# Late division in six 2-D attention heads, and the last two gate tiles as an eighth pair of block products

## The chip, the cores and the metric

The kernel runs on one core of one Trainium2 chip. The metric is the time of one execution on the device in microseconds (us); lower is better. The core has five engines that work through their own instruction lists in order: TensorE (PE, matrix products and transposes), VectorE (DVE), ScalarE (ACT), GpSimd (POOL) and SyncE (SP), which here only issues transfers (DMA). ACT issues some transfers too.

## The reference

One layer of an encoder on a sequence of 1024 positions of width 1024, all in float32. Two attentions with 8 heads of width 64 each run side by side on one projection of the same input, and their outputs are gated and summed:

```
h = rmsnorm(x) * (1 + scale1) + shift1
qa, ka, va, qb, kb, vb, ga, gb = split(h @ w_in)        # 6 x 512, then 2 x 1024 columns
oa = mixture_of_dilations(qa, ka, va)                   # 8 heads, 1-D windows
ob = neighbourhood_attention_2d(qb, kb, vb)             # 8 heads, 8 x 16 windows on a 16 x 64 grid
merged = sigmoid(ga) * (oa @ w_branch_dil) + sigmoid(gb) * (ob @ w_branch_na)
x = x + gate1 * (merged @ w_out)
...                                                     # then an up projection, a convolution, a down projection
```

In the 2-D attention each query row has its scores, a bias and a softmax over its window: `p = exp(s - max) / sum`, and `o = p @ v`. The division by the sum can stand before the product with v or behind it.

## The kernel before

Every product in full precision is made of three matmuls on halves of its operands: each float32 matrix is split into a high part (an ACT copy to a shorter format) and a low part (a subtraction on DVE or POOL), and high x high, high x low and low x high are summed in PSUM. The output of the projection is made transposed, in tiles of 128 columns of `w_in` by two halves of 512 positions. `w_in` has 40 such tiles; 24 to 39 are the gates.

The profiled execution falls into these stages (times from the trace):

- 0 to 143 us: the conditioning vector, the norm, and the products for the values.
- 143 to 276 us: the **block products**. Tiles of `w_in` are taken two at a time, as a pair, and the pair's product with `h` is made by a scheme with seven instead of eight block products (`STEPS`, `a_operands`, `products`). Seven pairs (`order = (4, 5, 6, 7, 1, 2, 3)`, the q and k tiles of both attentions) have 7 x 4 x 3 = 84 matmuls each. Their operands are sums and differences of blocks of the raw tiles, made by POOL and DVE and split by ACT and POOL while the pair before multiplies. Results leave PSUM through ACT and DVE (`na_evict`, `qk_evict`) into a tile `qs`, and from there go to `q_scr` in DRAM (the transfers `qks<-qs`).
- 276 to 282 us: nine units of the gates, as cover for the start of the attention.
- 282 to 610 us: the **attention**, a loop over slots numbered 0 to 101. Each slot has at most one block of scores `S` (PE), the transposes `T` of earlier softmax results (PE), and the products `O` with the values (PE). Slots 0 to 63 start the scores of the first attention, slots 64 to 95 those of the 2-D heads, four slots for each head (`NaHead(head, 64 + 4 * head)`). Between these PE does the gates as filling (`fill_steps`): 16 tiles of 2 halves of 8 units, where a **unit** is the three matmuls of lines L84, L85 and L86. The loop's number `n` says how many units a slot gets: 2 up to slot 63, 3 from 64 to 95, 1 behind. One unit stands ahead of S, the rest behind it. What is left comes behind the last slot.
- 610 to 710 us: the two branch products and the gating; then the output projection and the feed-forward part, which the change doesn't touch.

**One 2-D head.** The queries come in four blocks `cb`, in the order 0, 3, 1, 2, one a slot; I call these slots j = 0 to 3. Line L1260 makes two score matrices (R = 0, 1) of 128 queries by 288 keys (blocks 0 and 3) or 384 keys (1 and 2). Two slots of PSUM hold them. At the start of the next slot, `settle` runs the softmax: DVE adds the bias and takes the maximum (L1270), ACT takes the exponential and the row sums into `st[:, 1]` (L1272). Two slots behind the scores, `normalise` divides: DVE takes the reciprocal of two columns of sums (L1277), then POOL multiplies the R = 0 half of `P` and DVE the R = 1 half (L1280). Then PE transposes `P` in groups of four 128-column pieces (`turn`, L1289): per head six groups, in slots with two groups, one group, two groups, one group. The tile `T` has two PSUM banks. Each group leaves its bank through `split_t`: ACT copies the high part `th` (L878), DVE subtracts the low part `tl` (L882), and only then is the bank free.

The order inside `settle` is this: first all `th` copies of the turned groups (ACT), then the softmax of the scores just made (DVE, ACT), then the `tl` subtractions (DVE). So `tl` stands behind the softmax on DVE. `out` (L930) multiplies `th` and `tl` with the values, and an ACT copy (L1309) and a DVE addition (L1313) bring the result into `oTs[pair]`, a tile 128 x 1024 for two heads, which goes to `o_scr` in DRAM.

Other work of DVE, ACT and POOL in this stretch is queued with `aside(ns, one, two)` and handed out by `catch_up(550)` behind each unit: the splits of the gate weights (`whi` L961, `wlo` L962), of the values (`vv` L783, L784), the copies of finished gates (`gs`), the additions into `u`. SP's issues are written in the same slots: `bias`, `qs`, `ks`, `kl`, `vv` of a head come one head ahead; SP also carries the spreading of the merge weights of the first attention (`sts`, `fs`, `fcs`, `fb`), which ends in the first half of the 2-D heads.

Of the kernel before, what the change touches and what calls it, by code (L numbers as in the profile page):

```python
# [29 lines left out]
def hybrid_encoder(tc, xT, c, w_ada, small, w_in, p1_bias, p23_bias, na_bias, ln2_mult, ident, w_br, w_out,  # L30
# [8 lines left out]
    def f(ap):  # L39
        return ap.bitcast(FT)  # L40
# [240 lines left out]
    g_scr = dram.tile([16, 128, S], FT, name="gs")  # L281
    st_scr = dram.tile([4, 64, 128], FT, name="sts")
    f_scr = dram.tile([4, 2, 2, 8, S], FT, name="fcs")
    o_scr = [dram.tile([4, 128, S], FT, name=n) for n in ("oa", "ob")]
    v_scr = dram.tile([S + 9 * 128, 512], FT, name="v")
    va_s, va_b = v_scr[:S], v_scr[S:].rearrange("(j p) n -> j p n", j=9)
# [92 lines left out]
    def na_evict(pr, y, hf, p):  # L379
        first = (pr, y) not in na_st  # L380
        if first:
            na_st[pr, y] = [qkpool.tile([128, S], FR, name="qs") for _ in range(2)]
        st = na_st[pr, y]
        if y:
            split_qk(y, [t.rearrange("p (w t r) -> p r w t", w=16, t=16)[:, 2 * hf:2 * hf + 2] for t in st],
                     p.rearrange("p (r w t) -> p r w t", r=2, w=16))
        else:
            for r in range(2):
                split_qk(y, [t.rearrange("p (c w r t) -> p r c w t", c=4, w=16, r=4)[:, 2 * hf + r] for t in st],
                         p.rearrange("p (r w c t) -> p r c w t", r=2, w=16, c=4)[:, r])  # L390
        if not first:
            for x_, t in enumerate(na_st.pop((pr, y))):
                act.dma_start(q_scr[pr, 2 * y + x_], f(t))

    def qk_load(head):
        pr, i = divmod(head, 2)
# [129 lines left out]
    with tc.manual_schedule(engines={e.engine for e in (sp, act, dve, pool, pe)}):  # L526
# [176 lines left out]
            for c, d in ((c0, d0), (c1, d1)):  # L703
                pool.tensor_tensor(c, c, d, OP.subtract)

        order = (4, 5, 6, 7, 1, 2, 3)

        def p_load(n):
            pr, r = order[n], []
            for t in (pr, 4 + pr) if pr < 4 else (8 + pr, 12 + pr):  # L710
                r.append(wpool.tile([128, KT, 128], FT, name="wraw") if n % 2 == 0 and n < 6 else
                         lpool.tile([128, KT, 128], FT, name="xr", bufs=2))
                sp.dma_start(r[-1], w_in[t])
            return [t.rearrange("p (a b) m -> p a b m", a=2) for t in r]
# [95 lines left out]

    def p_products(n, seq=range(7)):
        pr = order[n]
        return products(p_sts[n], 4, p_moving, lambda i, hf, src: na_evict(pr, i, hf, src) if pr > 3 else
                        qk_evict(pr, i, hf, src, "qs"), seq, in_psum=True, other=lambda: p_spot([128, 2, 512])[:, 0])

    def advance(g):
        for j in g:
# [389 lines left out]
    class NaHead:  # L1207
        def __init__(self, head, s0):
            self.head, self.i = head, head % 2
            self.a = slice(64 * self.i, 64 * self.i + 64)  # L1210
            self.P, self.t3, self.bt = {}, {}, {}
            at(57 if head == 0 else s0 - 4, "first", lambda: qks.update({8 + head: qk_load(8 + head)}))
            at(s0, "first", self.begin)
            at(s0 + 2, "first", self.load)
            at(s0 + 6, "first", self.output)
            at(s0 + 5, "first", self.prepare)
            for n, cb in enumerate((0, 3, 1, 2)):
                at(s0 + n - 2, "first", self.bias, cb)
                at(s0 + n, "S", self.scores, cb)
                at(s0 + n + 2, "first", self.normalise, cb)  # L1220
            for n, pair in enumerate(((0, 3), (1, 2))):
                s = s0 + 4 + 2 * n
                for y in range(3):
                    at(s + (y == 2), "T", self.turn, pair, y)
                at(s + 3, "O", self.out, pair)
# [49 lines left out]
        def normalise(self, cb):  # L1275
            st, P, kn = self.st, self.P[cb], 48 * NA_NC[cb]
            dve.reciprocal(st[:, 1, 2 * cb:2 * cb + 2], st[:, 1, 2 * cb:2 * cb + 2])  # L1277
            for R in range(2):
                pp = P[:, R, :kn]
                (pool, dve)[R].tensor_scalar(pp, pp, st[:, 1, 2 * cb + R:2 * cb + R + 1], None, OP.mult)  # L1280

        def turn(self, pair, y):
            m = 16 * NA_NC[pair[0]]
            cb = pair[y % 2]
            spots = ([(cb, 0, 0), (cb, 1, 0), (cb, 1, 1), (cb, 3, 1)] if y < 2 else
                     [(pair[0], 2, 0), (pair[0], 2, 1), (pair[1], 2, 0), (pair[1], 2, 1)])
            pt = ps_a.tile([128, 512], FT, name="T")
            for x_, (cb, g, R) in enumerate(spots):
                pe.transpose(pt[:m, 128 * x_:128 * x_ + 128], self.P[cb][:, R, m * (g - R):m * (g - R) + m], idt)  # L1289
            split_t(pt, lambda tt: self.t3.update({(pair, y): tt}), m)  # L1290

        def out(self, pair):
            m = 16 * NA_NC[pair[0]]
            ensure(self.mark)
            t3 = [self.t3.pop((pair, y)) for y in range(3)]
            po = o_tile()
            for y, cb in enumerate(pair):
                turned_products(po, [(self.vv[:m, 4 * cb + g], [t[:m, c0:c0 + n] for t in tt],
                                      slice(256 * y + d0, 256 * y + d0 + n)) for g, tt, c0, d0, n in
                                     ((1, t3[y], 128, 0, 256), (2, t3[2], 256 * y, 0, 256), (0, t3[y], 0, 0, 128),  # L1300
                                      (3, t3[y], 384, 128, 128))], True)
            oT = oTs[self.head // 2]
            parts = [(oT[self.a].rearrange("p (r w t) -> p w r t", r=4, w=16)[:, :, :, 4 * cb:4 * cb + 4],
                      po[:, 256 * y:256 * y + 256].rearrange("p (w r t) -> p w r t", w=16, r=4))
                     for y, cb in enumerate(pair)]

            def one():
                for dst, pv in parts:
                    act.activation(dst, pv[64:128], AF.Copy)  # L1309

            def two():
                for dst, pv in parts:
                    dve.tensor_tensor(dst, pv[0:64], dst, OP.add)  # L1313
                if self.i and pair == (1, 2):
                    later(1, lambda: sp.dma_start(o_scr[1][self.head // 2], oT))
            o_marks.append(aside(800, one, two))

    def fill_steps():
        w, raw = first_w, {1: ahead.pop(25)}
# [11 lines left out]
        def release():  # L1331
            while held:
                args = held.pop()
                marks.append(aside(600, lambda: out(*args)))
        for n in range(16):
            ensure(w_mark)
            if n < 15:
                w_next = [wpool.tile([128, KT, 128], FR, name=x_) for x_ in ("whi", "wlo")]
                w_mark = side_split(raw.pop(n + 1), *w_next)
            if n < 14:  # L1340
                raw[n + 2] = ahead.pop(26) if n == 0 else w_load(w_in[26 + n])
            elif n == 14:
                w_raw[0] = w_load(w_br[0])
            for hf in range(2):
                ensure(marks[2 * n + hf])
                p = ps_g.tile([128, 512], FT, name="pj")
                for k in range(KT):
# [2 lines left out]
                        release()  # L1350
                    if k == KT - 1:
                        held.append((p, n, hf))
                        if n == 15 and hf:
                            release()
                    yield
            w = w_next

    oTs, w_raw = {}, {}
    for pr in range(4):
        DilPair(pr)  # L1360
    for head in range(8):
# [15 lines left out]
    fill(9)  # L1377
    for s in range(LAST + 1):
        now[0] = s
        n = 2 if s < 64 else 3 if s < 96 else 1  # L1380
        settle()
        run(slots[s]["early"])
        run(slots[s]["first"])
# [743 lines left out]
```

## Time and profile before

| | us |
|---|---|
| three timed runs | 1453.87, 1459.68, 1456.46 |
| their median | 1456.46 |
| the profiled execution | 1457.42 |
| its span in the trace | 1455.6 |
| PE busy, share of the span | 1430.4, 98% |
| DVE, ACT, POOL busy | 952.3, 793.0, 860.2 |
| mean granted TensorE clock | 0.998 |

The span is what the profile's instructions cover; the profiled execution's own time is 1.8 us longer. It is 1.0 us above the median of the timed runs.

In the profile's rows, "x8" joins eight equal instructions that follow each other, and the number in front is the time of the joined row; what stands in brackets is idle time of the engine ahead of the row and what ended it. Matmuls overlap: their distance from start to start is shorter than the duration shown. On PE the distance is what counts.

### The profile page before, as it was taken

The numbers are of one execution on the slowest core, as the hardware profiler recorded it, in microseconds if no ns is written. First come the engines' busy times: TensorE is split into PE (matmuls) and PEld (weight loads), VectorE is DVE, ScalarE is ACT, GpSimd is POOL, SyncE is SP. The second block draws the span as 40 slices with busy tenths as digits, with TensorE's granted clock in tenths as the row PEclk, the third lists the DMA queues.
The fourth block names the chain that finished last, engine by engine and source line by source line (L and its number), as shares of the span: only waits on it lengthen the run. The fifth ranks groups of instructions, "written<-read, shape, count | busy, mean of one in ns | idle before, by whom it ended". The sixth has DMA issues, their size and how long they took to land.

```text
span 1455.6 us, 21205 instructions
## 1 busy us (share of the span) xinstructions
PE 1430.4 (98%) x7276; PEld 1207.1 (83%) x7276; DVE 952.3 (65%) x1793; ACT 793.0 (54%) x1479; POOL 860.2 (59%) x707
## 2 busy tenths in 40 slices
PE   9999999999999999999999999999999999999998
PEld 8888788888888888887888778888888888887787
DVE  7687454365656766666418997666666668787865
ACT  6625543288887676644345554444444448575542
POOL 4156675343663675422478588677666676988712
PEclk9999999999999999999999999999999999999999
DMA  9587244676776797587444122222222233642313
GB/s 369 215 330 256 101 174 171 214 218 179 227 235 198 243 299 249 167 293 246 160 159 148 62 87 90 84 87 87 87 87 87 87 138 105 216 139 65 113 36 116
DMA packets 131498, 241.11 MB, mean 166 GB/s; under 512 B 48640, under 2 KB 62592, under 8 KB 131328
## 3 DMA queue, kind: packets, MB, share of 16 engines
q1 hardware_dynamic: 122304, 219.26, 46.0%
q10 hardware_dynamic: 9088, 20.52, 3.7%
q8 instruction: 57, 0.93, 0.3%
q14 instruction: 49, 0.40, 0.1%
HBM read 185.34 MB, written 60.16 MB: 169 GB/s over the span
## 4 chain that ended last, share of the span: by engine, by line
PE 71%; DVE 9%; DMA 7%; POOL 6%; ACT 3%; issue 3%; SPq 0%; ACTq 0%; DVEq 0%; POOLq 0%
PE pj L499 13%; PE pj L497 13%; PE pj L498 13%; PE pj L84 7%; PE pj L85 7%; PE pj L86 7%; PE O L930 3%; POOL wlo L61 2%; DMA oraw<-w_ada 2%; PE T L1289 1%; PE S L1260 1%; DMA wraw<-w_down 1%; PE T L1047 1%; DVE op L1661 1%; PE S L1070 1%
## 5 line engine op out<-in xcount | busy, mean ns | idle before, releaser
L61 POOL TENSOR_TENSOR wlo<-wraw,whi 128x512 fp32r<-128x512 f32 (+1 forms) x90 | 113.7, 1284 | 126.1 <-ACT whi L57 111.8
L497 PE MATMUL pj<-op,wsh 128*128 128x512 f32 x408 | 158.5, 390 | 1.6 <-ACT wsh L57 1.6
L498 PE MATMUL pj<-op,wsh 128*128 128x512 f32 x408 | 158.7, 389 | 0.4 <-DVE op L1550 0.4
L499 PE MATMUL pj<-op,wsl 128*128 128x512 f32 x408 | 157.4, 389 | 0.0
L61 POOL TENSOR_TENSOR wsl<-big,wsh 128x512 fp32r<-128x512 f32 (+1 forms) x86 | 111.7, 1320 | 45.0 <-ACT wsh L57 39.8
L84 PE MATMUL pj<-h,whi 128*128 128x512 f32 x272 | 115.1, 423 | 0.0
L86 PE MATMUL pj<-h,wlo 128*128 128x512 f32 x272 | 106.9, 393 | 0.0
L85 PE MATMUL pj<-h,whi 128*128 128x512 f32 x272 | 106.7, 392 | 0.0
L1760 DVE SCALAR_TENSOR_TENSOR big<-pj,sm,big 128x512 f32<-128x512 f32 (+2 forms) x183 | 94.9, 563 | 16.5 <-ACT big L1754 15.6
L497 PEld LDWEIGHTS pj<-op,wsh 128*128 128x128 f32 x408 | 76.6, 188 | 18.3 <-ACT wsh L57 2.4
L497 PE MATMUL pj<-op,whi 128*128 128x512 f32 x232 | 90.7, 391 | 0.3 <-ACT wc L503 0.3
L498 PE MATMUL pj<-op,whi 128*128 128x512 f32 x232 | 90.5, 390 | 0.2 <-DVE op L1580 0.2
L498 PEld LDWEIGHTS pj<-op,wsh 128*128 128x128 f32 x408 | 76.6, 188 | 16.9 <-DVE op L1550 0.9
L499 PE MATMUL pj<-op,wlo 128*128 128x512 f32 x232 | 90.3, 389 | 0.0
L499 PEld LDWEIGHTS pj<-op,wsl 128*128 128x128 f32 x408 | 76.6, 188 | 15.9 <-POOL wsl L61 0.2
L61 POOL TENSOR_TENSOR wsl<-wraw,wsh 128x384 fp32r<-128x384 f32 (+1 forms) x46 | 56.6, 1252 | 55.8 <-ACT wsh L57 50.2
L868 DVE CUSTOM_DVE_ANT_0 P<-S,bias 128x256 f32<-128x256 f32 x128 | 49.1, 421 | 61.2 <-PE S L1032 34.0
L882 DVE TENSOR_TENSOR tl<-T,th 128x512 fp32r<-128x512 f32 (+3 forms) x120 | 76.0, 649 | 8.6 <-ACT th L878 8.5
L57 ACT ACTIVATE whi<-wraw 128x1024 fp32r<-128x1024 f32 (+2 forms) x48 | 47.4, 992 | 57.7 <-PE pj L85 28.8
L869 ACT ACTIVATE P<-P,st 128x256 f32<-128x256 f32 x128 | 64.1, 502 | 26.0 <-DVE st L868 25.2
L962 POOL TENSOR_TENSOR wlo<-wraw,whi 128x512 fp32r<-128x512 f32 x30 | 38.6, 1294 | 64.6 <-ACT whi L961 61.1
L1754 ACT ACTIVATE big<-pj,sm 128x512 f32<-128x512 f32 x61 | 47.0, 772 | 54.3 <-DVE pj L518 32.2
(470 smaller groups left out, 4486.4 us busy)
## 6 DMA issues: line engine op xcount, KB each, us to landing
wada<-w_ada SPq DMA_DIRECT2D x31, 512.0 KB
qks<-qs ACTq DMA_DIRECT2D x28, 512.0 KB
wraw<-w_in SPq DMA_DIRECT2D x24, 512.0 KB
big<-w_up SPq DMA_DIRECT2D x22, 512.0 KB
wraw<-w_up SPq DMA_DIRECT2D x22, 512.0 KB
big<-as SPq DMA_DIRECT2D x22, 512.0 KB
as<-big SPq DMA_DIRECT2D x21, 512.0 KB
qs<-qks SPq DMA_DIRECT2D x32, 256.0 KB
```

The costliest lines, as they stand in the source:

```text
L57: act.activation(hi, raw, AF.Copy)
L61: lo_eng.tensor_tensor(lo[:, i:i + step], raw[:, i:i + step], f(hi)[:, i:i + step], OP.subtract)
L84: pe.matmul(psum, whi[:, k0 + k], mhi, start=k == 0, stop=False)
L85: pe.matmul(psum, whi[:, k0 + k], mlo, start=False, stop=False)
L86: pe.matmul(psum, wlo[:, k0 + k], mhi, start=False, stop=k == n - 1)
L497: pe.matmul(psum, whi[:, k], bhi, start=j < 4 and k == 0, stop=False, skip_group_check=True)
L498: pe.matmul(psum, whi[:, k], blo, start=False, stop=False, skip_group_check=True)
L499: pe.matmul(psum, wlo[:, k], bhi, start=False, stop=k == n - 1, skip_group_check=True)
L868: dve.tensor_tensor_reduce(pp, d, bias, -1.0, BIG, OP.add, OP.min, mi)
L869: act.activation(pp, pp, AF.Exp, bias=mi, scale=-1.0, accum_out=li)
L882: dve.tensor_tensor(tt[1][:m, :n], pt[:m, :n], f(tt[0])[:m, :n], OP.subtract)
L1760: dve.scalar_tensor_tensor(y[:, dst], src, wt, y[:, dst], OP.mult, OP.add)
```

## The change

It has three parts.

1. **Late division** in heads 0 to 5. `normalise` is no longer called for them. Instead, at slot s0 + 5 DVE takes the reciprocal of all eight columns of sums at once (`inverse`), a slot later SP stores the 1024 numbers to a new DRAM tensor `i_scr` (1024 pieces of 4 bytes), at s0 + 8 SP loads them back, spread over 64 partitions, into half of a 128 x 1024 tile `qb` (`load_inverse`, 256 KB), and behind the second head of a pair POOL multiplies the finished `oTs[pair]` by it in four pieces (`scale`, 128 x 256 each). The store of `oTs[pair]` to `o_scr` moves from behind the last addition to behind the fourth piece. Heads 6 and 7 divide as before.
2. **An eighth pair.** `order` gets an eighth entry, the gate tiles 38 and 39. They are loaded, prepared and multiplied like the other pairs, 84 matmuls ahead of the attention. `gate_evict` brings them to SBUF by plain ACT copies and stores each whole tile to `g_scr` by an ACT transfer.
3. **Fewer filling units.** `fill_steps` runs over 14 tiles instead of 16 (224 units instead of 256), and the slots 64 to 95 get two units instead of three. The loops behind the last slot have as many as before.

```diff
+    i_scr = dram.tile([8, S], FT, name="is")
...
+    def gate_evict(i, hf, p):
+        first = (8, i) not in na_st
+        if first:
+            na_st[8, i] = qkpool.tile([128, S], FT, name="qs")
+        act.activation(na_st[8, i][:, halves[hf]], p, AF.Copy)
+        if not first:
+            act.dma_start(g_scr[14 + i], na_st.pop((8, i)))
...
-        order = (4, 5, 6, 7, 1, 2, 3)
+        order = (4, 5, 6, 7, 1, 2, 3, 8)
...
-            for t in (pr, 4 + pr) if pr < 4 else (8 + pr, 12 + pr):
-                r.append(wpool.tile([128, KT, 128], FT, name="wraw") if n % 2 == 0 and n < 6 else
+            for t in (pr, 4 + pr) if pr < 4 else (8 + pr, 12 + pr) if pr < 8 else (38, 39):
+                r.append(wpool.tile([128, KT, 128], FT, name="wraw") if n % 2 == 0 else
...
-                at(s0 + n + 2, "first", self.normalise, cb)
+                if head > 5:
+                    at(s0 + n + 2, "first", self.normalise, cb)
+            if head < 6:
+                at(s0 + 5, "first", self.inverse)
+                at(s0 + 8, "early", self.load_inverse)
+                if self.i:
+                    for cb in range(4):
+                        at(s0 + 11 + cb // 2, "last", self.scale, cb)
...
+        def inverse(self):
+            st = self.st
+            dve.reciprocal(st[:, 1], st[:, 1])
+            later(1, lambda: sp.dma_start(i_scr[self.head].rearrange("(e p) -> p e", p=128), st[:, 1]))
+
+        def load_inverse(self):
+            if self.i == 0:
+                inv[self.head // 2] = qk2.tile([128, S], FT, name="qb")
+            sp.dma_start(inv[self.head // 2][self.a],
+                         i_scr[self.head].rearrange("(o n) -> o n", o=1).to_broadcast([64, S]))
+
+        def scale(self, cb):
+            ensure(self.done)
+            pr = self.head // 2
+            dst = oTs[pr].rearrange("p (r w t) -> p w r t", r=4, w=16)[:, :, :, 4 * cb:4 * cb + 4]
+            by = inv[pr][:, 256 * cb:256 * cb + 256].rearrange("p (w r t) -> p w r t", w=16, r=4)
+            pool.tensor_tensor(dst, dst, by, OP.mult)
+            if cb == 3:
+                later(1, lambda: sp.dma_start(o_scr[1][pr], oTs[pr]))
...
-        for n in range(16):
+        for n in range(14):
...
-        n = 2 if s < 64 else 3 if s < 96 else 1
+        n = 2 if s < 96 else 1
```

What this does to the instruction lists shows best at two places. The first is PE in the middle of the 2-D heads, from the scores of slot j = 3 to those of the next head's j = 0 (`T` are the transposes, `S` the scores, the rest are units of the gates). Before:

```order
L1260 MATMUL S<-kl,qs 128x384
L84 MATMUL pj<-h,whi 128x512
L85 MATMUL pj<-h,whi 128x512
L86 MATMUL pj<-h,wlo 128x512
L84 MATMUL pj<-h,whi 128x512
L85 MATMUL pj<-h,whi 128x512
L86 MATMUL pj<-h,wlo 128x512
L1289 MATMUL T<-idt,P 96x128 x8
L84 MATMUL pj<-h,whi 128x512
```

With the change:

```order
L1276 MATMUL S<-kl,qs 128x384
L84 MATMUL pj<-h,whi 128x512
L85 MATMUL pj<-h,whi 128x512
L86 MATMUL pj<-h,wlo 128x512
L1325 MATMUL T<-idt,P 96x128 x8
L84 MATMUL pj<-h,whi 128x512
```

Between the scores and the next two groups of transposes one unit stands where two stood; the same holds in each of the 32 slots. The unit behind the transposes and ahead of the next scores is as before.

The second place is DVE over one slot boundary of the same stretch, from the softmax (ISA) on slot j = 1's scores to the next softmax (`tl` frees a bank of `T`, `u` is the addition of an output). Before:

```order
L1270 ISA P,stb<-S,bias 128x288
L1270 ISA stb 128x1
L882 TENSOR_TENSOR tl<-T,th 96x512
L1277 RECIPROCAL stb<-stb 128x2
L1280 TENSOR_SCALAR P<-P,stb 128x288
L1313 TENSOR_TENSOR u_5824<-O,u_5824 64x16x4x4 x2
L1270 ISA P,stb<-S,bias 128x384
```

With the change:

```order
L1286 ISA P,stb<-S,bias 128x288
L1286 ISA stb 128x1
L891 TENSOR_TENSOR tl<-T,th 96x512
L1349 TENSOR_TENSOR u_5874<-O,u_5874 64x16x4x4 x2
L1286 ISA P,stb<-S,bias 128x384
```

The reciprocal and the multiplication that fall away stood behind `tl`; the softmax still stands ahead of it.

The third place is SP around head 2's first loads (`fs` belongs to the first attention, `vv`, `bias`, `qs` to head 2 and 3, `is` and `qb` are the reciprocals). Before:

```order
L402 DMA kl<-qks 64x1024 x2
L1327 DMA gs<-gs 128x512
L1149 DMA fs<-sts 64x2x32
L1153 DMA fs<-sts 8x2x32 x8
L777 DMA vv<-vb 96x4x64
L777 DMA vv<-vb 128x4x64 x2
L777 DMA vv<-vb 96x4x64
L1248 DMA bias<-na_bias 128x576 x2
L65 DMA wraw<-w_in 128x1024
L1248 DMA bias<-na_bias 128x768
```

With the change:

```order
L411 DMA kl<-qks 64x1024 x2
L1301 DMA is<-stb 128x8x1
L1364 DMA gs<-gs 128x512
L1158 DMA fs<-sts 64x2x32
L1162 DMA fs<-sts 8x2x32 x8
L786 DMA vv<-vb 96x4x64
L786 DMA vv<-vb 128x4x64 x2
L786 DMA vv<-vb 96x4x64
L1264 DMA bias<-na_bias 128x576 x2
L1306 DMA qb<-is 64x1024
L1264 DMA bias<-na_bias 128x768
```

Each of the six heads adds one store and one load to this queue; a third of the gate stretch's `wraw` loads and `gs` stores falls away.

More of the change, by code (lines that the diff above doesn't have):

```diff
@@ L812, in p_products @@
         pr = order[n]
-        return products(p_sts[n], 4, p_moving, lambda i, hf, src: na_evict(pr, i, hf, src) if pr > 3 else
-                        qk_evict(pr, i, hf, src, "qs"), seq, in_psum=True, other=lambda: p_spot([128, 2, 512])[:, 0])
+        return products(p_sts[n], 4, p_moving, lambda i, hf, src: gate_evict(i, hf, src) if pr > 7 else
+                        na_evict(pr, i, hf, src) if pr > 3 else qk_evict(pr, i, hf, src, "qs"), seq, in_psum=True, other=lambda: p_spot([128, 2, 512])[:, 0])
     def advance(g):
@@ L1313, in two @@
                     dve.tensor_tensor(dst, pv[0:64], dst, OP.add)
-                if self.i and pair == (1, 2):
+                if self.i and pair == (1, 2) and self.head > 5:
                     later(1, lambda: sp.dma_start(o_scr[1][self.head // 2], oT))
-            o_marks.append(aside(800, one, two))
+            self.done = aside(800, one, two)
+            o_marks.append(self.done)
     def fill_steps():
@@ L1334, in release @@
                 marks.append(aside(600, lambda: out(*args)))
-        for n in range(16):
+        for n in range(14):
             ensure(w_mark)
-            if n < 15:
+            if n < 13:
                 w_next = [wpool.tile([128, KT, 128], FR, name=x_) for x_ in ("whi", "wlo")]
                 w_mark = side_split(raw.pop(n + 1), *w_next)
-            if n < 14:
+            if n < 12:
                 raw[n + 2] = ahead.pop(26) if n == 0 else w_load(w_in[26 + n])
-            elif n == 14:
+            elif n == 12:
                 w_raw[0] = w_load(w_br[0])
@@ L1352, in fill_steps @@
                         held.append((p, n, hf))
-                        if n == 15 and hf:
+                        if n == 13 and hf:
                             release()
@@ L1356, in fill_steps @@
             w = w_next
-    oTs, w_raw = {}, {}
+    oTs, inv, w_raw = {}, {}, {}
     for pr in range(4):
```

## The prediction

> **What bounds the kernel now.** I read the page first (busy shares, slices, chain), then the stages by windows, then what PE waits for, then single slots.
>
> ```profile
> PE 1430.4 (98%) x7276; PEld 1207.1 (83%) x7276; DVE 952.3 (65%) x1793; ACT 793.0 (54%) x1479; POOL 860.2 (59%) x707
> PE 71%; DVE 9%; DMA 7%; POOL 6%; ACT 3%; issue 3%; SPq 0%; ACTq 0%; DVEq 0%; POOLq 0%
> ```
>
> PE is busy for 98% of the span, and 71% of the chain that ended last runs over it. So time is PE's list, plus the places where PE waits. The stages (block products; the 2-D heads, and two stretches of these) say the same, at a full clock, and the 2-D heads have the fuller transfers:
>
> ```profile
> 143.00:282.00 139.00, 137.18 (x603) 112.41 (x602) 62.08 (x89) 58.56 (x90) 80.61 (x63) 1.00 0.45 157
> 463.80:610.00 146.20, 142.00 (x930) 125.81 (x929) 98.49 (x293) 101.93 (x271) 87.12 (x77) 1.00 0.75 238
> 470.00:550.00 80.00, 77.74 (x500) 68.77 (x500) 57.67 (x174) 57.46 (x155) 51.67 (x46) 1.00 0.87 271
> 550.00:610.00 60.00, 58.06 (x392) 51.46 (x391) 37.31 (x109) 40.08 (x105) 32.90 (x30) 1.00 0.57 182
> ...
> PE T L1289 <- DVE stb L1277: 3.1, 3, 1.5
> ```
>
> The columns are window, length, busy us of PE, PEld, DVE, ACT and POOL, clock, DMA share, GB/s. The last row is from PE's waits between 463 and 612 us: in all of the 2-D heads PE lost only 3.1 us at the transposes, in three places. Neither DVE (98 of 146 us) nor POOL (87) bounds this stage; what they do matters only where PE waits for it.
>
> **The eighth pair adds 84 matmuls.** Their distance is read in a pair of before:
>
> ```profile
> 255.20 0.39 PE L497 MATMUL pj<-op,kl 128*128 128x512 f32 x1
> 260.64 0.39 PE L497 MATMUL pj<-op,kl 128*128 128x512 f32 x1
> PE pj L499 <- POOL kl L61: 1.2, 1, 1.2
> ```
>
> 24 matmuls lie between these two starts: 5.44 / 24 = 0.2267 us each, and 84 x 0.2267 = **+19.0**. The preparation on POOL, DVE and ACT runs beside the seventh pair (in this stage POOL is busy 81 of 139 us, ACT 59, the DMA share is 0.45). Without that cover a pair waits as the one that did, 1.2 us; I take 0 and keep +1.2. The new eviction is shorter than the one it stands behind (a plain copy), so the start of the attention is only moved.
>
> **32 units fall away.** Head 4 of before from its first scores to the next head's, with the slot boundary at its end (j = 3 to the next head's j = 0), PE and then DVE; then the boundary from j = 1 to j = 2:
>
> ```profile
> 530.68 0.29 PE L1260 MATMUL S<-ks,qs 128*128 128x288 f32 x1
> ...
> 543.27 0.34 PE L1260 MATMUL S<-ks,qs 128*128 128x384 f32 x1
> 543.98 0.40 PE L84 MATMUL pj<-h,whi 128*128 128x512 f32 x1
> 544.68 0.39 PE L84 MATMUL pj<-h,whi 128*128 128x512 f32 x1
> 545.37 1.04 PE L1289 MATMUL T<-idt,P 128*96 128x128 f32 x8
> 546.94 0.29 PE L1260 MATMUL S<-ks,qs 128*128 128x288 f32 x1
> ...
> 543.94 0.56 DVE L1270 CUSTOM_DVE_ANT_0 P<-S,bias 128x384 f32<-128x384 f32 x1
> 544.42 0.55 DVE L1270 CUSTOM_DVE_ANT_0 P<-S,bias 128x384 f32<-128x384 f32 x1
> 544.90 0.69 DVE L882 TENSOR_TENSOR tl<-T,th 128x512 fp32r<-128x512 f32 x1
> ...
> 537.04 1.04 PE L1289 MATMUL T<-idt,P 128*128 128x128 f32 x8
> ...
> 536.48 0.68 DVE L882 TENSOR_TENSOR tl<-T,th 96x512 fp32r<-96x512 f32 x1
> 537.08 0.15 DVE L1277 RECIPROCAL stb<-stb 128x2 f32<-128x2 f32 x1
> ```
>
> A unit is 544.68 - 543.98 = 0.70 us, and 32 x 0.70 = **-22.4**. With the pair that makes -3.4, near what twelve matmuls fewer (96 against 84) are worth, 2.7.
>
> **What the removed unit uncovered.** This is the term that decides the sign. In slots with two groups of transposes (j = 0 and j = 2), the first group takes the free bank of `T`, and the second needs the bank of the slot before, which is free when DVE's `tl` ends; and `tl` stands behind the softmax on the scores that PE has just made. The chain is: scores, two softmax passes, `tl`, second group. Its start is fixed by the scores, and between scores and transposes PE had two units and now has one. A group takes 0.44 us (the joined row of eight is 1.04, of four 0.60, below). For j = 0: the second group started at 545.37 + 0.44 = 545.81, `tl` ended at 544.90 + 0.69 = 545.59. For j = 2: 537.48 against 537.16. How soon behind `tl` can a group start? Where one waited:
>
> ```profile
> 500.69 2.68 DVE L1171 TENSOR_TENSOR fa<-fa,fl 64x32 f32<-64x32 f32 x2
> 504.05 0.68 DVE L882 TENSOR_TENSOR tl<-T,th 96x512 fp32r<-96x512 f32 x1
> 500.65 2.67 POOL L784 TENSOR_TENSOR vv<-vv 96x256 fp32r<-96x256 f32 x3
> 504.87 0.63 PE L1289 MATMUL T<-idt,P 128*128 128x128 f32 x4 [1.48 <-DVE stb L1277]
> 493.88 0.60 PE L1289 MATMUL T<-idt,P 128*96 128x128 f32 x4
> 495.27 0.62 PE L1289 MATMUL T<-idt,P 128*96 128x128 f32 x4 [0.79 <-DVE stb L1277]
> 563.03 0.61 PE L1289 MATMUL T<-idt,P 128*96 128x128 f32 x4 [0.80 <-DVE stb L1277]
> ```
>
> 504.87 - (504.05 + 0.68) = 0.14. (The profile names the reciprocal behind `tl`; the bank is what was late.) So the margin was 545.81 - 545.59 - 0.14 = 0.08 us in j = 0 and 0.18 in j = 2. With 0.70 less on PE the second group waits 0.62 and 0.52. There are 8 turns of the first kind and 7 of the second (behind the last head's there are no scores): 8 x 0.62 + 7 x 0.52 = **+8.6**. Single groups (j = 1, j = 3) take the bank that a two-group slot freed early; they wait nothing.
>
> Two of the three old waits are of the same kind (495.27 and 563.03): there ACT had split gate weights ahead of `th`. Such a wait cost 495.27 - (493.88 + 0.44) = 0.95 us. With fewer units these splits fall into other slots, where by the new order no second group stands right behind them: 2 x 0.95 = **-1.9**, and 0 if they only wander. The third, 504.87, comes from DVE, whose two small `fa` products took 2.68 us while POOL ran `vv`. This work stays, so I leave it at 0; -1.6 if it is gone.
>
> The Trainium skill ("SBUF — State Buffer", section "SBUF: two separate sides") says that DVE with two SBUF inputs and a GpSimd operation that reads SBUF share a port pair that is an exclusive lock: who comes second blocks for the whole instruction. The `fa` row beside the `vv` row agrees. By that rule, 24 POOL passes fewer would make such blocks rarer, the collision would go, and the sum would be 1.6 lower; but `tl` and the softmax each have an input in PSUM, so the rule would not shorten their chain.
>
> **Late division itself.** What goes and what comes, from the groups between 485 and 585 us:
>
> ```profile
> L1280 POOL TENSOR_SCALAR P<-P,stb 128x384 f32<-128x384 f32 x12 | 16.8, 1397 | 19.5 <-DVE stb L1277 9.4 <-ACT P L1272 7.7 <-DMA qs<-qks 1.3
> L1280 POOL TENSOR_SCALAR P<-P,stb 128x288 f32<-128x288 f32 x12 | 12.8, 1070 | 12.4 <-DVE stb L1277 12.4
> L784 POOL TENSOR_TENSOR vv<-vv 96x256 fp32r<-96x256 f32 x13 | 9.7, 743 | 0.0
> L1280 DVE TENSOR_SCALAR P<-P,stb 128x288 f32<-128x288 f32 x12 | 6.6, 551 | 0.4
> ```
>
> POOL loses 24 passes of 1.1 to 1.4 us and gets 12 of about 0.74 (`scale`, 128 x 256, nearest to `vv` 96 x 256); DVE loses 24 x (0.15 + about 0.5) and gets six reciprocals. On PE's path this is **0**, in both directions: DVE's reciprocal begins at 537.08, behind `tl`, so the chain above is as long without it. `scale` has a head's time for its input (five slots from store to use) and is done long before `oTs` is read behind 610 us.
>
> **Transfers.** SP's queue is in order, and this stretch of it runs without a pause:
>
> ```profile
> 472.19 0.48 SPq L1145 DMA_DIRECT2D sts<-fr  x1
> 492.56 0.90 SPq L1248 DMA_DIRECT2D bias<-na_bias  x2
> 496.98 0.46 DVE L1270 CUSTOM_DVE_ANT_0 P<-S,bias 128x288 f32<-128x288 f32 x1 [0.53 <-POOL P L1280]
> 504.90:507.10 2.20, 2.20 (x13) 2.02 (x14) 1.37 (x4) 0.89 (x3) 1.10 (x1) 1.00 0.26 26
> DMA packets 506, 0.06 MB, mean 26 GB/s; under 512 B 506, under 2 KB 506, under 8 KB 506
> ```
>
> Head 2's first bias is issued at 492.56 and its softmax ran at 496.98, 4.4 us later. The chain to that issue starts with a result of DVE (`sts`) and is 20.4 us long; with the change PE does the way from there to head 2 in some 4 us less (six slots by 0.70), so a bias that had one to two us of slack comes two to three late. In the stretch as a whole, the share of 0.87 over 80 us is 69.6 us of full transfers. By the terms so far a head shrinks from 16.26 us (546.94 - 530.68) by 4 x 0.70 - 1.14 = 1.66, a tenth, so 80 become 71.8. Each head's 256 KB more for `qb` are paid by the gate tiles that are no longer loaded and stored there. And the six stores of 1024 pieces: 506 small packets took 0.26 x 2.2 us of all engines, 1.1 ns each, so 1024 take 1.2 us and the five of this stretch 5.8. 69.6 + 5.8 = 75.4 us of full transfers do not go into 71.8. What is loaded ahead (q and k of a head are issued during the head before) takes some of it. From below this is 0 (all hidden), from above 8.2 (80 - 71.8: the stretch keeps its length). I take **+3.0**, nearest to the 3.6 that are missing.
>
> The Trainium skill ("DMA: Bandwidth & Descriptors", section "Specifications") asks for at least 512 B a transfer for line rate, with a read-modify-write below it, which speaks against the 4-byte store; no row here shows 4-byte packets, so my 1.2 us comes from the small ones that are there.
>
> **The sum** against the profiled execution: 1457.4 + 19.0 - 22.4 + 8.6 - 1.9 + 3.0 = 1463.7. It stood 1.0 above the median of the runs: **1462.7**.
>
> **Rivals.**
>
> - *The turns do not wait.* If DVE gets to `tl` earlier than in the rows above, or the granularity of my margin (0.08 and 0.18 us) is wrong, +8.6 goes; the old waits may go too. For it speaks that DVE and POOL have less to do and that an emptier DVE can only help; against it, that in the rows `tl` (544.90) began as the second pass of the softmax (544.42 + 0.55) ended, and the first pass 0.67 us behind the first scores, so nothing but the chain itself held them. Profiled 1457.4 + 19.0 - 22.4 - 1.9 = 1452.1 to 1455.1 with the transfers' 3.0, or 1450.5 without the collision: a median of 1449.5 to 1454, I say 1452.
> - *Transfers hold the 2-D heads* (the slower side). The place is SP's queue and the DMA engines from 470 to 550 us; it decides when the 75.4 us of transfers, by what stands in front of them, are needed in order. Then 3.0 becomes 8.2: 1468.9 profiled, **1467.9** median. For it: the share of 0.87 already, the small packets, the late bias. Against it: only 182 GB/s behind 550 us, so what is late can be caught up, and the lead of q and k.
> - *The pair does not come free of waits:* +1.2, inside the ranges.
>
> **How the numbers follow.** The forecast has 0.50, no waits 0.22, transfers 0.28. A measurement of this kernel tells a change from none at about 0.5%, 7.3 us: below 1449.2 is faster, above 1463.7 slower. The forecast's own range is 1457 (turns at half their price) to 1466 (old waits wander, pair waits); of its 0.50 I put 0.20 above 1463.7, none below 1449.2. Of the 0.22 without waits, 0.08 are faster; of the 0.28, 0.25 are slower. So faster 0.08, within 0.47, slower 0.45. The range that should hold 8 of 10 runs from 1451 (near the case without waits) to 1470 (the transfers' case with the pair's wait).
>
> **What would show it.** Right: PE's distance per head falls from 16.26 to some 14.6 us; in the waits of PE in the 2-D heads the second groups of transposes stand with 10 to 17 waits on DVE, 0.5 to 0.6 us each; the block products end 19 us later; DVE and POOL are emptier by 15 and 20 us with no gain from it. The transfers' term shows as waits of DVE's softmax on `bias`, or of S on `ks` and `qs`, between 465 and 560 us. Wrong: no waits at the transposes and heads of 13.5 us (the first rival), or heads of 16 us with DMA at a share near 1 (the second). A wait at the start of the attention, or between the pairs, would be a part that I put at nothing.

## The result: 50 us slower, and the profile after

| | before | with the change |
|---|---|---|
| median of the timed runs, us | 1456.19 (6 runs, 1453.87 to 1459.68) | 1506.14 (6 runs, 1501.82 to 1511.13) |
| span of the profiled execution, us | 1455.6 | 1509.3 |
| mean granted TensorE clock | 0.998 | 0.983 |

The ratio is 1.0337, with a 95% interval from 1.0319 to 1.0355. The forecast was 1462.7 us with a range up to 1470: the time went the forecast way, and almost eight times as far (50 us against 6.5).

The page with the change: busy shares, and the slices of PE's clock and of the transfers. Each slice is a fortieth of the span, 38 us.

```profile
PE 1443.9 (96%) x7264; PEld 1216.3 (81%) x7264; DVE 941.4 (62%) x1757; ACT 796.0 (53%) x1480; POOL 845.5 (56%) x701
PEclk9999999999999987999999999999999999999999
```

PE does the 12 matmuls fewer that were announced (7264 instead of 7276), but is busy 13 us longer, and in two slices its clock is lower. By stages, from the same views as before (window, length, busy us of PE, PEld, DVE, ACT, POOL, clock, DMA share, GB/s), and PE's waits from 480 to 640 us:

```profile
143.00:300.00 157.00, 155.16 (x684) 127.78 (x683) 65.67 (x96) 65.86 (x100) 94.13 (x74) 1.00 0.43 151
300.00:482.00 182.00, 179.17 (x1155) 158.34 (x1154) 108.52 (x377) 144.50 (x396) 93.84 (x86) 1.00 0.71 209
482.00:660.00 178.00, 133.14 (x817) 115.60 (x815) 83.54 (x251) 98.50 (x263) 62.53 (x62) 0.88 0.85 190
...
PE T L1325 <- DVE tl L891: 37.3, 14, 12.6
PE S L1276 <- DMA kl<-qks: 5.5, 1, 5.5
```

All of it lies in the 2-D heads. The first scores of head 0 come 20.0 us later than before (486.36 against 466.41 us); from there the head distances tell the rest. They are the distances between the first scores (S) of consecutive heads, from the rows of that line:

| head | 0 | 1 | 2 | 3 | 4 | 5 | 6 |
|---|---|---|---|---|---|---|---|
| before | 14.02 | 15.99 | 17.98 | 16.28 | 16.26 | 17.25 | 16.25 |
| with the change | 11.54 | 14.72 | 22.24 | 22.07 | 25.56 | 28.60 | 20.38 |

Head 0 is 2.5 us shorter, of the 2.8 that its four units are worth. From head 2 on every head is 4 to 11 us longer. One of the stops with the change, at the end of head 4, in the order of its causes: SP, the rate of the transfers, DVE, PE, and PE's clock.

```profile
575.74 0.38 SPq L1301 DMA_DIRECT2D is<-stb  x1
576.37 11.17 SPq L786 DMA_DIRECT2D vv<-vb  x4
587.59 0.95 SPq L1264 DMA_DIRECT2D bias<-na_bias  x2
...
GB/s 393 406 346 231 216 195 124 17 8 6 30 18 8 32 7 11 3 24 108 58 35 4 11 68 44 43 61 15 50 77 269 253 265 392 439 406 198 232 248 306
...
596.29 0.46 DVE L1286 CUSTOM_DVE_ANT_0 P<-S,bias 128x288 f32<-128x288 f32 x1 [15.09 <-issue]
597.05 1.28 DVE L891 TENSOR_TENSOR tl<-T,th 96x512 fp32r<-96x512 f32 x2
...
597.87 1.06 PE L1325 MATMUL T<-idt,P 128*96 128x128 f32 x4 [12.57 <-DVE tl L891]
...
585.30:597.80 12.50, 0.00 (x1) 0.00 (x0) 1.51 (x6) 1.01 (x4) 4.92 (x4) 0.59 0.82 128
597.80:601.00 3.20, 3.13 (x12) 2.84 (x13) 0.91 (x3) 1.55 (x5) 2.68 (x3) 0.50 1.03 304
```

The store of the reciprocals is issued at 575.74 us. The row of GB/s covers 576 to 600 us in slices of 0.6: by 580.2 the transfers have fallen from 400 GB/s to 17, and they stay between 3 and 108 until 594. The four loads of `vv` behind the store take SP 11.17 us to issue instead of two, so the bias of the next head goes out at 587.59. The softmax of the next head's first scores starts at 596.29 (for this one the profile names no releaser; for five others with the change, 27.0 us of waits, it names the bias), `tl` behind it, the bank of `T` behind that, and PE has stood for 12.57 us. When it starts again its clock is at 0.50 for 3.2 us. Behind each of the six stores PE stands in a like way, in the rows of `T` and S for 5.4, 5.4, 5.5 and 2.1, 12.6, 4.4 and 3.6 us.

### The profile page after: what moved, and what is told of

Read it like the earlier page. It is cut to its first block, busy times and chain, and to the rows that moved or that the text cites. A ratio compares the mean times of both kernels' runs of the same rounds, so it can differ in the third digit from the quotient of the medians.

```text
span 1509.3 us, 21166 instructions
## 1 busy us (share of the span) xinstructions
PE 1443.9 (96%) x7264; PEld 1216.3 (81%) x7264; DVE 941.4 (62%) x1757; ACT 796.0 (53%) x1480; POOL 845.5 (56%) x701
## 4 chain that ended last, share of the span: by engine, by line
PE 49%; DVE 3%; ACT 2%; POOL 2%; issue 1%; DMA 1%; DVEq 0%; POOLq 0%; ACTq 0%
PE pj L506 11%; PE pj L507 11%; PE pj L508 11%; PE pj L86 5%; PE pj L84 5%; PE pj L85 5%; ACT op L1616 1%; DMA wraw<-w_down 1%; DVE big L471 0%; POOL wsl L61 0%; POOL wlo L61 0%; DVE op L1698 0%; POOL big L453 0%; ACT wsh L57 0%; PE pcol L108 0%
## 5 line engine op out<-in xcount | busy, mean ns | idle before, releaser
L84 PE MATMUL pj<-h,whi 128*128 128x512 f32 x240 | 105.2, 438 | 0.0
L86 PE MATMUL pj<-h,wlo 128*128 128x512 f32 x240 | 96.6, 403 | 0.0
L85 PE MATMUL pj<-h,whi 128*128 128x512 f32 x240 | 96.3, 401 | 0.0
L793 POOL TENSOR_TENSOR vv<-vv 128x512 fp32r<-128x512 f32 (+2 forms) x40 | 43.1, 1093 | 90.8 <-ACT vv L792 90.8
L1286 DVE CUSTOM_DVE_ANT_0 P<-S,bias 128x288 f32<-128x288 f32 (+1 forms) x64 | 30.3, 505 | 78.7 <-DMA bias<-na_bias 32.6
```

Source lines behind the costliest of these rows:

```text
L84: pe.matmul(psum, whi[:, k0 + k], mhi, start=k == 0, stop=False)
L85: pe.matmul(psum, whi[:, k0 + k], mlo, start=False, stop=False)
L86: pe.matmul(psum, wlo[:, k0 + k], mhi, start=False, stop=k == n - 1)
```

## The experiments

**Theory A:** the store of 1024 pieces of 4 bytes stops all transfers for several us, six times. **Theory B:** the shorter slots bring every head's loads too late, as the prediction's second rival had it, whatever the store looks like. C and D are named in the expectations.

### The store by itself, and the change without it

Run e1: the change, with the reciprocals in another order in DRAM, and the scaling adapted to it.

```diff
-            later(1, lambda: sp.dma_start(i_scr[self.head].rearrange("(e p) -> p e", p=128), st[:, 1]))
+            later(1, lambda: sp.dma_start(i_scr[self.head].rearrange("(p e) -> p e", p=128), st[:, 1]))
...
-            by = inv[pr][:, 256 * cb:256 * cb + 256].rearrange("p (w r t) -> p w r t", w=16, r=4)
-            pool.tensor_tensor(dst, dst, by, OP.mult)
+            for R in range(2):
+                dst = oTs[pr].rearrange("p (r w t) -> p w r t", r=4, w=16)[:, 8 * R:8 * R + 8, :, 4 * cb:4 * cb + 4]
+                by = inv[pr].rearrange("p (w r t e) -> p e w r t", e=8, r=4, t=4)[:, 2 * cb + R]
+                pool.tensor_tensor(dst, dst, by, OP.mult)
```

> The changed kernel, but the reciprocals lie in DRAM with the eight numbers of a partition side by side: 128 pieces of 32 bytes a store instead of 1024 of 4 bytes. The bytes, the load (4096 contiguous bytes, spread over 64 partitions) and the number of issues are the same; GpSimd reads the numbers with a stride, in eight smaller passes a pair instead of four. Theory A (each store of 4-byte pieces holds up the transfers behind it for 8 us or more, and this is where the 50 us went): the first scores of consecutive 2-D heads come 14 to 15.5 us apart, no wait over 2 us at the transposes, a time of 1457 to 1463 us. Theory B (the shorter slots alone bring the loads of a head too late, whatever the store): above 1490 us, waits of 4 to 12 us at the transposes as in the changed kernel. Theory C (the lower granted clock seen in the changed kernel costs the time, the waits follow): clock below 0.99 and above 1480 us.

Measured: 1466.83 us, ratio 1.0070 [1.0043, 1.0098]. 39 of the 50 us are gone with the layout of one small store; B and C fall. It is 4 us above A's range, and the longest wait at the transposes is 2.4 us where A allowed 2: 10 us stay.

Run e2: the pair and the shorter slots, no late division.

```diff
-                if head > 5:
+                if True:
                     at(s0 + n + 2, "first", self.normalise, cb)
-            if head < 6:
+            if False:
                 at(s0 + 5, "first", self.inverse)
```

> The eighth pair and the slots with two units, and all eight heads divide early as before: no reciprocal is stored or loaded. Theory A: the transfers are then as before, and what remains of the prediction's sum is the pair 19.0, the units -22.4, the new waits at the second groups of transposes 8.6 and the old waits -1.9, so +3.3: 1456.2 + 3.3 = 1459.5 us, with 10 to 15 waits of 0.3 to 0.6 us at the transposes. Theory B: above 1490 us as the changed kernel. If the turns do not wait: 1451 us.

Measured: 1465.94 us, 1.0071 [1.0056, 1.0087]; +10.5 where 3.3 was expected. So as much is left with late division (e1) as without it. That does not make late division free: e1 trades one wait for another. The softmax waits longer for biases (9.3 us between 500 and 610 us, 5.4 in e2), but the two small `fa` products on DVE, which took 2.68 us beside `vv` on POOL before and 2.65 in e2, take 0.28 in e1, where `vv` runs at another time.

Run e3: late division alone, with the seven pairs, the 16 gate tiles and the three units of before.

```diff
-        order = (4, 5, 6, 7, 1, 2, 3, 8)
+        order = (4, 5, 6, 7, 1, 2, 3)
...
-        for n in range(14):
+        for n in range(16):
...
-        n = 2 if s < 96 else 1
+        n = 2 if s < 64 else 3 if s < 96 else 1
```

> Late division in six heads with the 4-byte stores, but seven pairs, 16 gate tiles and three units a slot as before. Theory A: the stores hold up the transfers as in the changed kernel, with 0.7 us more a slot to hide it (11 us for four slots of four heads): 1480 to 1500 us, with waits of several us at the transposes. Theory B (the shorter slots make the loads late): 1453 to 1459 us.

Measured: 1493.08 us, 1.0261 [1.0242, 1.0281]. The stops are there with the long slots too, 38 us of them.

Run e4: the kernel before, and six stores that nobody reads.

```diff
+            if head < 6:
+                at(s0 + 6, "first", self.keep)
...
+        def keep(self):
+            st = self.st
+            sp.dma_start(i_scr[self.head].rearrange("(e p) -> p e", p=128), st[:, 1])
```

> The kernel before, and nothing added but the six stores of the row sums in 1024 pieces of 4 bytes, issued in slot s0 + 6 of heads 0 to 5; nobody reads them. The division is as before. Theory A: 1480 to 1500 us, since the store by itself holds up what is behind it. Theory D (it is the load that waits for the store, and SP's queue behind that load): 1456 to 1460 us. By the price that the prediction put on a store (1.2 us of all engines), it would be within 1454 to 1462 us.

Measured: 1491.07 us, 1.0244 [1.0222, 1.0266]: +35.6 us, 5.9 us a store. Theory A holds, D falls, and the prediction's price (1.2 us of the engines, hidden beside the rest) is refuted. The rate of the transfers from 489 to 505 us in slices of 0.4 us, the store being issued at 489.91:

```profile
GB/s 3 2 5 46 3 6 1 0 0 22 19 0 0 0 0 1 12 69 25 9 19 21 26 18 20 18 41 20 19 58 110 208 275 334 253 259 395 406 414 429
```

From 490.6 to 500.6 us the rate stays between 0 and 69 GB/s, though loads of `vv` (issued from 490.39 on) and biases (from 493.78) stand in the queue.

### What about the store stops the transfers

Run e7: as e4, with 128 pieces of 32 bytes.

```diff
-            sp.dma_start(i_scr[self.head].rearrange("(e p) -> p e", p=128), st[:, 1])
+            sp.dma_start(i_scr[self.head].rearrange("(p e) -> p e", p=128), st[:, 1])
```

> The kernel before with six stores of row sums that nobody reads, as in the run with six stores, but laid out so that a partition's eight numbers lie side by side: 128 pieces of 32 bytes each. If the cost of a store goes with its number of small pieces (5.9 us for 1024), 128 pieces cost 0.7 us: 6 x 0.7, at most 1460 us, and no stretch without transfers. If it is the bare issue in this place of SP's queue that costs, 1485 to 1495 us as there.

Measured: 1459.55 us, 1.0018 [1.0003, 1.0033]: 0.4 us a store.

Run e8: as e4, still 1024 pieces of 4 bytes, but 64 bytes apart in DRAM.

```diff
-    i_scr = dram.tile([8, S], FT, name="is")
+    i_scr = dram.tile([8, S, 16], FT, name="is")
...
-            sp.dma_start(i_scr[self.head].rearrange("(e p) -> p e", p=128), st[:, 1])
+            sp.dma_start(i_scr[self.head].rearrange("(e p) o -> p e o", p=128)[:, :, 0:1],
+                         st[:, 1].rearrange("p (e o) -> p e o", o=1))
```

> As the run with six stores: 1024 pieces of 4 bytes a store, but each number 64 bytes from the next in DRAM instead of 4. If the stop comes from many pieces written to neighbouring addresses (16 of them in 64 bytes, from 16 different partitions), the pieces now go as fast as they are handed out, and the time is 1456 to 1462 us. If it comes from the number or the size of the pieces alone, 1485 to 1495 us as before.

Measured: 1457.60 us, 0.9998 [0.9983, 1.0014]: free. So neither the number of pieces nor their size is enough to cost anything. The same view as above, from 491 to 507 us, store at 491.98:

```profile
GB/s 0 5 5 6 1 7 2 0 60 181 253 286 286 271 219 351 380 422 383 389 371 379 384 423 405 394 410 379 348 369 236 318 389 410 379 328 97 122 77 48
```

Two us after the store the loads run again. Three more spacings ask how near is too near. Run e11: 16 bytes apart, against e8:

```diff
-    i_scr = dram.tile([8, S, 16], FT, name="is")
+    i_scr = dram.tile([8, S, 4], FT, name="is")
```

> As the run with six stores of 1024 pieces of 4 bytes, each number 16 bytes from the next in DRAM, so that 64 bytes hold four numbers (from four partitions) where they held sixteen, or one in the run 64 bytes apart. If pieces that share 64 bytes go one behind another, the stop is a few us in place of ten, and the time 1457 to 1470 us. If any sharing costs the whole stop, 1485 to 1495 us; if only touching neighbours cost, 1456 to 1460 us.

Measured: 1457.96 us, 1.0009 [0.9995, 1.0022]: free within the interval, so sharing 64 bytes does not by itself cost the stop.

Run e12: 8 bytes apart, the eight numbers of a partition behind each other, against e8:

```diff
-    i_scr = dram.tile([8, S, 16], FT, name="is")
+    i_scr = dram.tile([8, S, 2], FT, name="is")
...
-            sp.dma_start(i_scr[self.head].rearrange("(e p) o -> p e o", p=128)[:, :, 0:1],
+            sp.dma_start(i_scr[self.head].rearrange("(p e) o -> p e o", p=128)[:, :, 0:1],
```

> As the run with six stores, 1024 pieces of 4 bytes, but the eight numbers of one partition are 8 bytes apart and fill 64 bytes of their own: eight pieces share 64 bytes, and all come from one partition. If it matters that pieces of different partitions meet in the same 64 bytes, this is free: 1456 to 1460 us. If the sharing itself costs, whoever writes: 1465 to 1495 us.

Measured: 1476.33 us, 1.0135 [1.0115, 1.0156]: 3.4 us a store. It does not help that the pieces of a 64-byte stretch come from one partition.

Run e13: 8 bytes apart, neighbours from different partitions, against e8:

```diff
-    i_scr = dram.tile([8, S, 16], FT, name="is")
+    i_scr = dram.tile([8, S, 2], FT, name="is")
```

> As the run with six stores of 1024 pieces of 4 bytes, each number 8 bytes from the next in DRAM, neighbours from different partitions: eight pieces share 64 bytes as in the run where the eight of a partition had 64 bytes of their own (1476.3), but they come from eight partitions. If the number of pieces in 64 bytes sets the stop, 1470 to 1482 us, as there. If that run was slow since one partition's pieces follow each other into the same place, 1456 to 1465 us here.

Measured: 1463.25 us, 1.0044 [1.0030, 1.0059]: 1.1 us a store. This is in the second range: the same density costs less when neighbours come from different partitions. It is not free, though the pieces do not touch. So the stop grows as the pieces lie denser (64 and 16 bytes apart 0, 8 bytes 1.1, 4 bytes 5.9 us, all in the order of e4), and at the same density one partition's pieces behind each other cost more (3.4) than those of eight partitions (1.1). What in the path to DRAM does this is not settled by these runs.

### The 10 us that are left

With two units behind the scores the prediction's margin comes back. Run e9: as e2, and in slots 64 to 95 both units behind the scores.

```diff
-        fill(n > 1)
+        k = n > 1 and s < 64
+        fill(k)
         run(slots[s]["S"])
         run(slots[s]["last"])
-        fill(n - (n > 1))
+        fill(n - k)
```

> The eighth pair and two units a slot, all heads dividing early, and in slots 64 to 95 both units behind the scores, none ahead of them (the amount of work is the same). Then 1.4 us lie between scores and transposes again. If the regular waits of 0.34 and 0.45 us at the second groups (0.50 and 0.61 from start to start) are the chain scores, softmax, tl, bank, as the prediction has it, these 14 waits go: 8 us less than with one unit ahead, 1456 to 1459 us, heads of 13.5 us. If PE waits in some other place instead (scores that need their banks, outputs that need tl), 1463 to 1467 us.

Measured: 1461.69 us, 1.0030 [1.0018, 1.0042], against 1.0071 [1.0056, 1.0087] for e2. The ratio is 0.0041 lower, 6 us, where 8 were expected; the time lies between the two ranges. One end of head and one middle of head in e2, then the same two turns in e9 (`T` x8 is a turn without a wait):

```profile
530.63 0.60 PE L1325 MATMUL T<-idt,P 128*96 128x128 f32 x4
531.68 0.61 PE L1325 MATMUL T<-idt,P 128*96 128x128 f32 x4 [0.45 <-DVE stb L1293]
537.82 0.60 PE L1325 MATMUL T<-idt,P 128*128 128x128 f32 x4
538.76 0.63 PE L1325 MATMUL T<-idt,P 128*128 128x128 f32 x4 [0.34 <-DVE stb L1293]
```

```profile
535.04 1.03 PE L1325 MATMUL T<-idt,P 128*128 128x128 f32 x8
541.97 1.04 PE L1325 MATMUL T<-idt,P 128*96 128x128 f32 x8
528.92 0.61 PE L1325 MATMUL T<-idt,P 128*96 128x128 f32 x4 [0.79 <-DVE stb L1293]
```

The second groups in e2 start 1.05 and 0.94 us behind the first instead of 0.44: waits of 0.61 and 0.50, where the prediction had 0.62 and 0.52. In e9 they are gone, and head 3 falls from 14.69 to 13.47 us. What e9 keeps is irregular: waits of 0.8 us at the end of three heads, as the last row, which is of the old kind (ACT's split of gate weights, L970, ran from 526.79 for 0.63 us ahead of `th`, and `tl` waited 0.40 us for that), and those of heads 1 and 2. The largest is 3.28 us at 520.99: the `fa` products ran beside `vv` there too, for 2.63 us, ahead of the softmax and `tl`. Head 2 of e2 is shown below. The head distances:

| head | 0 | 1 | 2 | 3 | 4 | 5 | 6 |
|---|---|---|---|---|---|---|---|
| e2 | 11.55 | 15.08 | 20.14 | 14.69 | 14.70 | 15.65 | 14.73 |
| e9 | 11.18 | 14.55 | 19.18 | 13.47 | 14.48 | 15.15 | 14.45 |

The largest piece of the rest of e2's 10 us is head 2, which is 2.2 us longer than before where it should have been 1.7 shorter. PE's waits there, the softmax behind its bias, and windows with the clock (third from the end):

```profile
516.19 0.46 DVE L1286 CUSTOM_DVE_ANT_0 P<-S,bias 128x288 f32<-128x288 f32 x1 [3.45 <-DMA bias<-na_bias]
517.78 0.61 PE L1325 MATMUL T<-idt,P 128*96 128x128 f32 x4 [2.27 <-DVE tl L891]
519.89 2.65 DVE L1180 TENSOR_TENSOR fa<-fa,fl 64x32 f32<-64x32 f32 x2
524.04 0.63 PE L1325 MATMUL T<-idt,P 128*128 128x128 f32 x4 [1.74 <-DVE stb L1293]
...
515.50:517.80 2.30, 0.03 (x2) 0.05 (x2) 1.61 (x6) 1.11 (x5) 0.00 (x0) 1.00 1.02 367
517.80:519.40 1.60, 1.60 (x7) 1.31 (x8) 1.53 (x6) 1.60 (x5) 0.91 (x1) 0.67 1.19 390
519.40:521.60 2.20, 2.20 (x8) 1.84 (x7) 2.13 (x3) 0.05 (x1) 2.20 (x3) 0.50 0.87 313
```

Head 2's bias is late by 3.45 us for the softmax, as the prediction's transfers term had it for this very load, without any store. Behind the wait of 2.27 us the granted clock is lower, 0.67 and 0.50 over the next 3.8 us, which is 1.6 x 0.33 + 2.2 x 0.50 = 1.6 us of matmul time more. Then the two `fa` products collide with POOL's `vv` (519.86 us, 2.64 long) as before, and PE waits 1.74 us.

Run e5: e1 with both units behind the scores (the edit of e9).

> All of the change, with the 32-byte layout of the reciprocals, and both units behind the scores in slots 64 to 95. By the same chain 7 to 8 us less than the 32-byte layout alone (1466.8): 1458 to 1460 us. Its remaining waits (the late biases behind the 256 KB loads) may grow, since PE gets to them earlier: then 1461 to 1465 us.

Measured: 1468.43 us, 1.0058 [1.0038, 1.0079], the same as e1 within the intervals, though both ranges were below it. (The five runs stand at two levels, 1462.7 and 1463.3, and three at 1468.4 to 1468.7; the ratio lies between.) The waits go from the turns to the loads: the waits of DVE's softmax between 500 and 610 us, e1 first, then e5:

```profile
DVE P L1286 <- DMA bias<-na_bias: 9.3, 3, 3.6
```

```profile
DVE P L1286 <- DMA bias<-na_bias: 17.8, 6, 4.5
```

Run e10: as e5, the loads of the reciprocals behind the biases and a slot later.

```diff
-                at(s0 + n - 2, "first", self.bias, cb)
+                at(s0 + n - 2 - (n == 2), "first", self.bias, cb)
...
-                at(s0 + 8, "early", self.load_inverse)
+                at(s0 + 9, "last", self.load_inverse)
...
-                        at(s0 + 11 + cb // 2, "last", self.scale, cb)
+                        at(s0 + 13 + cb // 2, "last", self.scale, cb)
```

> The whole change with 32-byte pieces and both units behind the scores (1468.4 us), and the order of SP's loads changed: the 256 KB of reciprocals are loaded a slot later, behind that slot's biases and q and k, the scaling follows two slots later, and the third bias of a head is loaded a slot earlier. If what is left there (17.8 us of waits of the softmax on biases) comes from the 256 KB ahead of the biases in the queue, the biases come in time and the time is 1459 to 1463 us, that of the pair alone with both units behind (1461.7). If the transfer engines are simply full in this stretch, something else comes late and it stays at 1465 to 1470 us.

Measured: 1468.25 us, 1.0081 [1.0057, 1.0105], no better; the softmax still waits 13.2 us for biases (490 to 610 us). This order in the queue is not it; that the transfers of this stretch are full is what remains of the two answers, though no run here took bytes away to show it. No version tried is faster than the kernel before.

## Why the prediction was wrong

- **The pair, +19.0.** Right: head 0's first scores moved by 20.0 us with the change (19.7 in e2's execution, 486.07 - 466.41). No wait was added between the pairs, and the attention began without one.
- **The units, -22.4, and the turns, +8.6.** Right in mechanism and size: 0.61 and 0.50 us a turn in e2, heads of 14.7 us where 14.6 was said, and 13.47 in e9 when the second unit stood behind the scores again. The rival without waits at the turns is refuted by the same rows.
- **The old waits, -1.9.** Wrong where it can be seen, in e9: three heads have such a wait (0.79 to 0.81 us in the brackets), where before had two (0.79 and 0.80). They did not go, they wandered, the other end that the prediction had named (0). In e2 they mostly don't show, since the regular wait covers them. The third old wait, left at 0, is 1.74 us in e2 and 3.28 in e9 where it was 1.48. The collision behind it goes where there is late division, as one sentence of the prediction had it: `fa` takes 0.28 us in the change and in e1, with no `vv` beside it. Whether the passes that fall away or only the shifted times did it, no run separates.
- **Late division itself, 0.** Even without the costly store it is 0 only as a balance: e1 and e2 are equal (1.0070 and 1.0071), with the longer waits for biases against the collision that is gone. Where the turns no longer wait it costs something: e10 has 1.0081 [1.0057, 1.0105] against 1.0030 [1.0018, 1.0042] for e9, some 7 us, with 13.2 us of waits for biases against 4.2 (500 to 610 us). (e5, with 1.0058, has an interval that touches that of e9.)
- **Transfers, +3.0.** This is the step that failed, in its smallest part. The prediction priced a store by the time that small packets took the engines, "1.1 ns each, so 1024 take 1.2 us and the five of this stretch 5.8". Those packets were of some 120 bytes each (0.06 MB in 506). Measured: 5.9 us a store in the kernel before (e4), (1506.1 - 1466.8) / 6 = 6.6 in the change. It is not the time on the engines that was too small: in e4, 918 small packets between 490.9 and 491.9 us took 43.1% of all engines, 0.47 ns each. The price lies in what the prediction had no term for, the ten us behind them in which the other transfers hardly move. The other parts of the term, the late bias of head 2 and a full stretch, are seen in e2 (3.45 us) and in e5.
- **The bound from above, 8.2** ("the stretch keeps its length") was no bound: it supposed that transfers only take turns, and that the stretch could at worst stay as long as before. A transfer that stops the others makes it longer. The rival on the slower side named the right place, SP's queue and the transfers from 470 to 550 us, and had a price some six times too small: 8.2 us, where (1506.1 - 1456.2) - 3.3 = 46.6 lie beyond the pair, the units, the turns and the old waits as forecast.
- **The clock** was taken as 1.00 throughout. In the 2-D heads it is 0.88 with the change (the windows above): PE was busy for 133.14 us with 817 instructions there, 163 ns each. The same stage of e2:

```profile
482.00:622.00 140.00, 126.92 (x847) 110.95 (x846) 100.70 (x297) 100.86 (x268) 83.36 (x74) 0.99 0.75 238
```

  That is 150 ns each, so about 817 x 13 ns = 11 us of the loss are matmuls at a lower clock, by an estimate that takes the mix of matmuls in the two windows as equal. Standing still makes the larger part: 178.0 - 133.1 = 44.9 us against 13.1.

The Trainium skill had a warning that the prediction did not draw on. "DMA: Bandwidth & Descriptors", section "Rules for kernel authors", says that a strided last dimension becomes one descriptor for each element, and to rearrange so that it is contiguous. The runs agree that this store was the thing to avoid (e4), and e8, with as many single numbers 64 bytes apart, shows that it is where they land in DRAM that costs, not their number.

## What to carry to other kernels

A store of single numbers is priced by where the numbers land, not by its bytes or its count: 4 KB in adjacent 4-byte pieces held up the transfers for ten us, and the same 1024 pieces 16 or 64 bytes apart, or 128 pieces of 32 bytes, cost nearly nothing. If a view of before has no row for a new kind of transfer, its upper bound is not that of the nearest transfer; put such a store alone into the old kernel first, which is one run. And filling that is taken out between a producer and its consumer gives back only what the consumer's chain leaves: here 1.1 of 2.8 us a head went to the turns, until the units were put where the chain is.

## What the runs showed of the hardware

- Behind one store of 1024 adjacent 4-byte pieces the core's transfers, all queues together, stay between 0 and 69 GB/s for ten us (e4), while in e8, with the pieces 64 bytes apart, they are back at 181 GB/s within three us. The cost of a store depends on the distance of its pieces in DRAM and on their order: 5.9 us at 4 bytes, 1.1 at 8 bytes, 3.4 at 8 bytes with a partition's eight behind each other, 0.2 at 16 bytes (not told from 0) and 0 at 64.
- A wait of 2.3 us can be followed by a lower clock on PE: behind 515.5 to 517.8 us in e2 it was granted 0.67, then 0.50 for together 3.8 us (the windows above), which cost 1.6 us more than the wait's row says. It is not a matter of the length alone: behind waits of 3.28 us in e9 (at 520.99), 2.44 in e10 (at 520.33) and 2.29 in e13 (at 505.46) the clock stayed at 1.00. The Trainium skill ("TensorE: Matmul & The Clock Gate", section "Part 1: The HAM clock gate (the "warmup" mystery)") puts the change to half the clock after an idle window of about 3.4 us; here a shorter wait was followed by it in e2, and one of nearly that length was not in e9.
- The two small DVE products `fa` took together 2.68, 2.65 and 2.63 us where `vv` ran on POOL at the same time (before, e2, e9), and 0.28 where it did not (the change, e1).
